# RMSNorm with SiLU on one core: framework-placed waits, a ring of 96 rows and 2 MB transfers in place of a critical section with hand-placed waits and 1 MB transfers

## The chip, the cores and the metric

The kernel runs on 1 core of one Trainium2 chip. Four of its engines appear below: ACT (ScalarE) and DVE (VectorE) do most of the arithmetic (120.5 and 112.0 us busy before), POOL (GpSimd) the reciprocal roots (32 of 1427 ns), and SP (SyncE) issues the transfers, which the core's 16 DMA engines carry out. The metric is device time in microseconds (us). An execution of the kernel before takes 166.9 us with a spread of about 0.3%. The "span" that a profile quotes is the measured stretch of one profiled execution, about 1.8 us shorter than the time of that run.

"1 MB" is 2^20 bytes throughout, "2 MB" 2^21.

## The reference, cut to what matters

```python
# x: (16, 1024, 512) float32, gamma: (512,) float32, eps: 1e-5
def reference(x, gamma, eps):
    rms = np.sqrt(np.mean(x ** 2, axis=-1, keepdims=True) + eps)
    x_norm = x / rms * gamma
    return (x_norm * (1.0 / (1.0 + np.exp(-x_norm)))).astype(np.float32)
```

There are 16384 rows of 2 KB, 32 MB in and 32 MB out. Every byte is read once and written once, whatever the kernel.

## The kernel before

Rows are handled in tiles of 128 partitions x 4 rows, which is 1 MB. There are 32 tiles and 20 buffers ("slots"). Everything sits in one critical section, a region in which the framework adds no waits between the instructions, so every wait and every semaphore (a counter that one engine raises and another waits for, as ACT and SyncE do with `s_swish` below) is written by hand.

```python
    n = 4
    n_act = 3
    lead = 8
    slots = 20
    T = R // (P * n)
    xv = xf.rearrange("(t p n) d -> t p n d", p=P, n=n)      # one partition: 4 rows = 8 KB in a row
    # ...
    def load(t):
        if t >= slots:
            nc.sync.wait_ge(st[t % slots], 16 * (t // slots))
        nc.sync.dma_start(out=X(t), in_=xv[t]).then_inc(ld[t % slots], 16)

    def store(t):
        nc.sync.wait_ge(s_swish, t + 1)
        nc.sync.dma_start(out=ov[t], in_=X(t)).then_inc(st[t % slots], 16)
    # ... ACT: 3 squares with row sums; DVE: 1 square, mean + eps, 4 x (x * rstd * gamma);
    # ... POOL: power -0.5; ACT: Silu on the whole tile
    with tc.tile_critical():
        for t in range(lead):
            load(t)
        for t in range(T):
            store(t)
            if t + lead < T:
                load(t + lead)
        # ... ACT:  sum_act(t), then swish(t - 2)
        # ... DVE:  sum_dve(t), mean_eps(t), then norm(t - 1)
        # ... POOL: root(t)
        for s in range(slots):
            nc.sync.wait_ge(st[s], 16 * ((T - 1 - s) // slots + 1))
```

SyncE (SP) issues all big transfers from one queue: 8 loads first, then store, load, store, load, each of 1 MB.

## Time and profile before

| | before |
|---|---|
| time, median of 4 runs beside the change | 166.87 us (166.76 to 167.04) |
| span of the profiled run | 165.0 us |
| busiest compute engine | ACT, 73% of the span |
| first DMA packet, last DMA packet (from the trace's DMA records) | 1.95 us, 162.14 us |

These are lines of the page of the kernel before. Each digit of the DMA row is the busy share of the 16 DMA engines in one fortieth of the span, in tenths; below it stands what they moved in that slice.

```profile
span 165.0 us, 713 instructions
...
DVE 112.0 (68%) x226; ACT 120.5 (73%) x225; POOL 46.4 (28%) x38
...
DMA  4999999999999999999999999999999999999990
GB/s 157 415 425 429 425 342 429 411 431 427 427 431 419 431 423 433 423 431 425 429 427 427 423 425 431 421 435 419 435 423 431 425 425 431 421 433 423 433 405 26
DMA packets 9229, 67.16 MB, mean 407 GB/s; under 512 B 1028, under 2 KB 1028, under 8 KB 1032
...
q1 hardware_dynamic: 9216, 67.11, 97.0%
```

The row of nines says that the DMA engines work from the first load to the last store. ACT and DVE have a quarter of their time or more to spare. The kernel is bound by DMA; the one sag, a dip of that rate (342 GB/s, the sixth slice), is where the first store reaches the engines.

The lines of the page on the chain that ended last, on the two largest groups on ACT, and on the transfers (count, KB, median us from issue to landing):

```profile
DMA xb<-in_x_dram 63%; ACT junk_a L86 12%; ACT xb L129 6%; DVE xb L121 5%; SPq L79 1%; SPq L75 0%; DVE aeps L107 0%; SPq L203 0%; SPq L131 0%
...
L86 ACT ACTIVATE junk_a<-xb 128x512 bf16<-128x512 f32 x96 | 59.2, 617 | 26.9 <-DMA xb<-in_x_dram 26.9
...
L129 ACT ACTIVATE xb<-xb 128x2048 f32<-128x2048 f32 x32 | 60.6, 1895 | 2.2 <-DVE xb L121 2.2
...
xb<-in_x_dram SPq DMA_DIRECT2D x32, 1024.0 KB, 23.2
out_dram<-xb SPq DMA_DIRECT2D x32, 1024.0 KB, 22.4
```

The chain that ended last is for 63% of the span the landing of loads. A transfer lands 22 to 23 us after its issue, although 1 MB takes about 2.45 us (2452 or 2453 ns from one transfer to the next in the DMA records). So some 9 MB are queued ahead (22.4 or 23.2 us over 2.45 us per MB, an estimate from the medians). As long as that stays so, I took it that no wait on ACT, DVE or SyncE reaches the total, only the DMA engines' own work, the start and the end.

SyncE's issues in order of time (start, length, what), first and last:

```profile
0.94 4.15 SPq L75 DMA_DIRECT2D xb<-in_x_dram  x8
15.29 0.35 SPq L79 DMA_DIRECT2D out_dram<-xb  x1
...
122.18 30.42 SPq L79 DMA_DIRECT2D out_dram<-xb  x8
```

```profile
L131 SPq EVENT_SEMAPHORE  x3: 17/17/28, 163.5 to 163.8; - x3
L131 SPq NOP  x2: 13/13/13, 0.7 to 163.8; - x2
L131 SPq COMPARE_BRANCH  x1: 33/33/33, 163.1 to 163.1; - x1
```

### The profile page before, as it was taken

The numbers are of one execution on the slowest core, as the hardware profiler recorded it, in microseconds if no ns is written. First come the engines' busy times: TensorE is split into PE (matmuls) and PEld (weight loads), VectorE is DVE, ScalarE is ACT, GpSimd is POOL, SyncE is SP. The second block draws the span as 40 slices with busy tenths as digits, with TensorE's granted clock in tenths as the row PEclk, the third lists the DMA queues.
The fourth block names the chain that finished last, engine by engine and source line by source line (L and its number), as shares of the span: only waits on it lengthen the run. The fifth ranks groups of instructions, "written<-read, shape, count | busy, mean of one in ns | idle before, by whom it ended". The sixth has DMA issues, their size and how long they took to land.

```text
span 165.0 us, 713 instructions
## 1 busy us (share of the span) xinstructions
DVE 112.0 (68%) x226; ACT 120.5 (73%) x225; POOL 46.4 (28%) x38
## 2 busy tenths in 40 slices
DVE  0269999999996666786666776666876666784000
ACT  3488999999977977777977758877778977777000
POOL 1053334443333311333321233312333311330000
DMA  4999999999999999999999999999999999999990
GB/s 157 415 425 429 425 342 429 411 431 427 427 431 419 431 423 433 423 431 425 429 427 427 423 425 431 421 435 419 435 423 431 425 425 431 421 433 423 433 405 26
DMA packets 9229, 67.16 MB, mean 407 GB/s; under 512 B 1028, under 2 KB 1028, under 8 KB 1032
## 3 DMA queue, kind: packets, MB, share of 16 engines
q1 hardware_dynamic: 9216, 67.11, 97.0%
q14 instruction: 5, 0.04, 0.1%
q10 hardware_dynamic: 8, 0.01, 0.0%
HBM read 33.56 MB, written 33.55 MB: 407 GB/s over the span
## 4 chain that ended last, share of the span: by engine, by line
DMA 63%; ACT 17%; issue 6%; DVE 5%; SPq 1%
DMA xb<-in_x_dram 63%; ACT junk_a L86 12%; ACT xb L129 6%; DVE xb L121 5%; SPq L79 1%; SPq L75 0%; DVE aeps L107 0%; SPq L203 0%; SPq L131 0%
## 5 line engine op out<-in xcount | busy, mean ns | idle before, releaser
L121 DVE SCALAR_TENSOR_TENSOR xb<-xb,rstd,gamma_sb 128x512 f32<-128x512 f32 x128 | 87.4, 745 | 0.0
L86 ACT ACTIVATE junk_a<-xb 128x512 bf16<-128x512 f32 x96 | 59.2, 617 | 26.9 <-DMA xb<-in_x_dram 26.9
L114 POOL TENSOR_TENSOR rstd<-aeps,neg_half 128x4 f32<-128x4 f32 x32 | 45.7, 1427 | 99.4 <-DVE aeps L107 99.4
L129 ACT ACTIVATE xb<-xb 128x2048 f32<-128x2048 f32 x32 | 60.6, 1895 | 2.2 <-DVE xb L121 2.2
L97 DVE CUSTOM_DVE_ANT_0 junk_v<-xb 128x512 bf16<-128x512 f32 x32 | 22.0, 689 | 8.7 <-DMA xb<-in_x_dram 6.8
L107 DVE TENSOR_SCALAR aeps<-ms 128x4 f32<-128x4 f32 x32 | 5.4, 170 | 29.6 <-ACT junk_a L86 28.9
L86 ACT ACTIVATION_READ_ACCUMULATOR junk_a<-xb 128x1 f32 x96 | 17.9, 186 | 0.0
L146 ACT ACT_TABLE_LOAD x1 | 1.3, 1283 | 2.6 <-issue 2.6
L97 DVE DVE_READ_ACCUMULATOR2_ANT ms<- 128x1 f32 x32 | 2.6, 82 | 0.0
L162 DVE STREAM_SHUFFLE gamma_sb<-gamma 128x512 f32<-128x512 f32 x1 | 0.7, 717 | 0.0
L141 POOL MEMSET gamma<- 128x512 f32 x1 | 0.5, 524 | 0.5 <-PEq L203 0.5
L189 POOL MEMSET const-float32-0.0<- 128x1 f32 x1 | 0.1, 99 | 0.2 <-issue 0.2
L189 POOL MEMSET const-uint8-127<- 128x1 uint8 x1 | 0.1, 102 | 0.0
L147 POOL MEMSET neg_half<- 128x4 f32 x1 | 0.1, 102 | 0.0
L189 POOL MEMSET const-bfloat16-1.0<- 128x1 bf16 x1 | 0.1, 101 | 0.0
L189 POOL MEMSET const-float32-1.0<- 128x1 f32 x1 | 0.1, 98 | 0.0
L162 DVE LOAD_MASK_SELECT gamma_sb<-gamma x1 | 0.0, 13 | 0.0
## 6 DMA issues: line engine op xcount, KB each, us to landing
xb<-in_x_dram SPq DMA_DIRECT2D x32, 1024.0 KB, 23.2
out_dram<-xb SPq DMA_DIRECT2D x32, 1024.0 KB, 22.4
gamma<-in_gamma_dram ACTq DMA_DIRECT2D x1, 8.0 KB
```

The source lines that it names most:

```text
L79: nc.sync.dma_start(out=ov[t], in_=X(t)).then_inc(st[t % slots], 16)
L86: ins = nc.scalar.activation(out=junk_a[:, j, :], in_=X(t)[:, j, :], func=AF.Square, accum_out=ms[:, t, j : j + 1],)
L97: ins = nc.vector.tensor_tensor_reduce(out=junk_v[:, j, :], in0=X(t)[:, j, :], in1=X(t)[:, j, :], scale=1.0, scalar=0.0, op0=ALU.mult, op1 ...
L107: nc.vector.tensor_scalar(out=aeps[:, t, :], in0=ms[:, t, :], scalar1=inv_d, scalar2=eps_f, op0=ALU.mult, op1=ALU.add,).then_inc(s_aeps, 1)
L114: nc.gpsimd.tensor_tensor(out=rstd[:, t, :], in0=aeps[:, t, :], in1=neg_half[:], op=ALU.pow).then_inc(s_rstd, 1)
L121: ins = nc.vector.scalar_tensor_tensor(out=X(t)[:, j, :], in0=X(t)[:, j, :], scalar=rstd[:, t, j : j + 1], in1=gamma_sb[:], op0=ALU.mult, ...
L129: nc.scalar.activation(out=X(t), in_=X(t), func=AF.Silu).then_inc(s_swish, 1)
L141: nc.gpsimd.memset(gamma4[:], 0.0).then_inc(s_const, 1)
L146: nc.scalar.preload_act_table_set("silu_and_others")
L147: nc.gpsimd.memset(neg_half[:], -0.5).then_inc(s_half, 1)
L162: nc.vector.stream_shuffle(gamma_sb[:], gamma4[:], [0] * 32).then_inc(s_gamma, 1)
L189: nc = _bacc.Bacc("TRN2", target_bir_lowering=False, num_devices=1)
```

## The change

Its intent: let the framework place the waits (in the order in which the program is written, with no critical section), so that the hand-made semaphores go; make transfers larger (2 MB, a partition's run of 16 KB) while compute stays in pieces of 1 MB; keep 96 rows per partition in one ring; keep all transfers on SyncE.

```diff
-    n = 4
-    n_act = 3
-    lead = 8
-    slots = 20
+    sizes = [4, 4] + [8] * 15
+    ring = 96
+    ahead = 32
+    cn = 4
+    n_act = 3
...
     def load(t):
-        if t >= slots:
-            nc.sync.wait_ge(st[t % slots], 16 * (t // slots))
-        nc.sync.dma_start(out=X(t), in_=xv[t]).then_inc(ld[t % slots], 16)
+        nc.sync.dma_start(out=buf(t), in_=dram(xf, t))
 
     def store(t):
-        nc.sync.wait_ge(s_swish, t + 1)
-        nc.sync.dma_start(out=ov[t], in_=X(t)).then_inc(st[t % slots], 16)
+        nc.sync.dma_start(out=dram(of, t), in_=buf(t))
...
-    with tc.tile_critical():
+    with tc.manual_schedule():
...
+        while rows_loaded < ahead:
+            load(loaded)
+            ...
+        for k in range(K + 2):
+            if k < K:
+                sums(k)
+                root(k)
...
+            if 1 <= k <= K:
+                norm(k - 1)
+            if k >= 2:
+                swish(k - 2)
+                while stored < len(tiles) and ends[stored] <= k - 1:
+                    store(stored)
+                    stored += 1
+                    if loaded < len(tiles):
+                        load(loaded)
+                        loaded += 1
...
-        for s in range(slots):
-            nc.sync.wait_ge(st[s], 16 * ((T - 1 - s) // slots + 1))
```

Each direction now has 2 transfers of 1 MB and 15 of 2 MB. The order of instructions on ACT, DVE and POOL is the same as before.

More of the change, by code (lines that the diff above doesn't have):

```diff
@@ L27 @@
     R, D = xf.shape
-    n = 4
+    sizes = [4, 4] + [8] * 15
+    ring = 96
+    ahead = 32
+    cn = 4
     n_act = 3
-    lead = 8
-    slots = 20
-    T = R // (P * n)
-    assert T * P * n == R, (R, n)
-    xv = xf.rearrange("(t p n) d -> t p n d", p=P, n=n)
-    ov = of.rearrange("(t p n) d -> t p n d", p=P, n=n)
+    N = sum(sizes)
+    assert N * P == R, (N, R)
+    tiles = []
+    done = 0
+    for sz in sizes:
+        assert done % ring + sz <= ring
+        tiles.append((done * P, sz, done % ring))
+        done += sz
@@ L39 @@
+    chunks = [r for _, sz, at in tiles for r in range(at, at + sz, cn)]
+    K = len(chunks)
     pool = ctx.enter_context(tc.tile_pool(name="all", bufs=1))
-    xb = pool.tile([P, slots, n, D], fp32, name="xb")
+    junk_pool = ctx.enter_context(tc.tile_pool(name="junk", bufs=1))
+    xb = pool.tile([P, ring, D], fp32, name="xb")
     gamma4 = pool.tile([P, D], fp32, name="gamma4")
     gamma_sb = pool.tile([P, D], fp32, name="gamma_sb")
-    junk_a = pool.tile([P, n, D], bf16, name="junk_a")
@@ L44 @@
-    junk_v = pool.tile([P, n, D], bf16, name="junk_v")
-    neg_half = pool.tile([P, n], fp32, name="neg_half")
-    ms = pool.tile([P, T, n], fp32, name="ms")
-    aeps = pool.tile([P, T, n], fp32, name="aeps")
-    rstd = pool.tile([P, T, n], fp32, name="rstd")
+    neg_half = pool.tile([P, cn], fp32, name="neg_half")
+    ms = pool.tile([P, K, cn], fp32, name="ms")
+    aeps = pool.tile([P, K, cn], fp32, name="aeps")
+    rstd = pool.tile([P, K, cn], fp32, name="rstd")
     inv_d = 1.0 / float(D)
@@ L51 @@
     eps_f = float(eps)
-    ld = [tc.alloc_semaphore(f"ld{s}") for s in range(slots)]
-    st = [tc.alloc_semaphore(f"st{s}") for s in range(slots)]
-    g_ld = tc.alloc_semaphore("g_ld")
-    s_const = tc.alloc_semaphore("s_const")
-    s_half = tc.alloc_semaphore("s_half")
-    s_gamma = tc.alloc_semaphore("s_gamma")
-    s_sum_a = tc.alloc_semaphore("s_sum_a")
-    s_sum_v = tc.alloc_semaphore("s_sum_v")
-    s_aeps = tc.alloc_semaphore("s_aeps")
-    s_rstd = tc.alloc_semaphore("s_rstd")
-    s_norm = tc.alloc_semaphore("s_norm")
@@ L64, with dram, buf @@
-    s_swish = tc.alloc_semaphore("s_swish")
-    def X(t):
-        return xb[:, t % slots]
-    def landed(eng, t):
-        eng.wait_ge(ld[t % slots], 16 * (t // slots + 1))
+    def dram(ap, t):
+        first, sz, _ = tiles[t]
+        return ap[first : first + P * sz].rearrange("(p n) d -> p n d", n=sz)
+    def buf(t):
+        _, sz, at = tiles[t]
+        return xb[:, at : at + sz, :]
     def load(t):
-        if t >= slots:
-            nc.sync.wait_ge(st[t % slots], 16 * (t // slots))
-        nc.sync.dma_start(out=X(t), in_=xv[t]).then_inc(ld[t % slots], 16)
+        nc.sync.dma_start(out=buf(t), in_=dram(xf, t))
@@ L77, in store @@
     def store(t):
-        nc.sync.wait_ge(s_swish, t + 1)
-        nc.sync.dma_start(out=ov[t], in_=X(t)).then_inc(st[t % slots], 16)
-    def sum_act(t):
-        landed(nc.scalar, t)
-        if t > 0:
-            nc.scalar.wait_ge(s_sum_a, t)
-        for j in range(n_act):
-            ins = nc.scalar.activation(
-                out=junk_a[:, j, :], in_=X(t)[:, j, :], func=AF.Square,
-                accum_out=ms[:, t, j : j + 1],
-            )
-        ins.then_inc(s_sum_a, 1)
-    def sum_dve(t):
-        landed(nc.vector, t)
-        if t > 0:
-            nc.vector.wait_ge(s_sum_v, t)
-        for j in range(n_act, n):
-            ins = nc.vector.tensor_tensor_reduce(
-                out=junk_v[:, j, :], in0=X(t)[:, j, :], in1=X(t)[:, j, :],
-                scale=1.0, scalar=0.0, op0=ALU.mult, op1=ALU.add,
-                accum_out=ms[:, t, j : j + 1],
-            )
-        ins.then_inc(s_sum_v, 1)
@@ L104, in mean_eps, with sums @@
-    def mean_eps(t):
-        nc.vector.wait_ge(s_sum_a, t + 1)
-        nc.vector.wait_ge(s_sum_v, t + 1)
+        nc.sync.dma_start(out=dram(of, t), in_=buf(t))
+    def sums(k):
+        for j in range(cn):
+            row = xb[:, chunks[k] + j, :]
+            if j < n_act:
+                junk = junk_pool.tile([P, D], bf16, name=f"junk_a{j}")
+                nc.scalar.activation(
+                    out=junk[:], in_=row, func=AF.Square,
+                    accum_out=ms[:, k, j : j + 1],
+                )
+            else:
+                junk = junk_pool.tile([P, D], bf16, name=f"junk_v{j}")
+                nc.vector.tensor_tensor_reduce(
+                    out=junk[:], in0=row, in1=row,
+                    scale=1.0, scalar=0.0, op0=ALU.mult, op1=ALU.add,
+                    accum_out=ms[:, k, j : j + 1],
+                )
@@ L107, in mean_eps, with root @@
+    def root(k):
         nc.vector.tensor_scalar(
-            out=aeps[:, t, :], in0=ms[:, t, :], scalar1=inv_d, scalar2=eps_f,
+            out=aeps[:, k, :], in0=ms[:, k, :], scalar1=inv_d, scalar2=eps_f,
             op0=ALU.mult, op1=ALU.add,
-        ).then_inc(s_aeps, 1)
-    def root(t):
-        nc.gpsimd.wait_ge(s_aeps, t + 1)
+        )
         nc.gpsimd.tensor_tensor(
-            out=rstd[:, t, :], in0=aeps[:, t, :], in1=neg_half[:], op=ALU.pow
-        ).then_inc(s_rstd, 1)
-    def norm(t):
-        nc.vector.wait_ge(s_rstd, t + 1)
-        for j in range(n):
-            ins = nc.vector.scalar_tensor_tensor(
-                out=X(t)[:, j, :], in0=X(t)[:, j, :], scalar=rstd[:, t, j : j + 1],
+            out=rstd[:, k, :], in0=aeps[:, k, :], in1=neg_half[:], op=ALU.pow
+        )
@@ L123, in norm @@
+    def norm(k):
+        for j in range(cn):
+            row = xb[:, chunks[k] + j, :]
+            nc.vector.scalar_tensor_tensor(
+                out=row, in0=row, scalar=rstd[:, k, j : j + 1],
                 in1=gamma_sb[:], op0=ALU.mult, op1=ALU.mult,
             )
-        ins.then_inc(s_norm, 1)
-    def swish(t):
-        nc.scalar.wait_ge(s_norm, t + 1)
-        nc.scalar.activation(out=X(t), in_=X(t), func=AF.Silu).then_inc(s_swish, 1)
-    with tc.tile_critical():
-        for t in range(lead):
-            load(t)
-        for t in range(T):
-            store(t)
-            if t + lead < T:
-                load(t + lead)
-        nc.gpsimd.memset(gamma4[:], 0.0).then_inc(s_const, 1)
-        nc.scalar.wait_ge(s_const, 1)
-        nc.scalar.dma_start(
-            out=gamma4[0:P:32, :], in_=gamma.partition_broadcast(4)
-        ).then_inc(g_ld, 16)
-        nc.scalar.preload_act_table_set("silu_and_others")
-        nc.gpsimd.memset(neg_half[:], -0.5).then_inc(s_half, 1)
-        nc.gpsimd.wait_ge(s_half, 1)
-        for t in range(T + 2):
-            if t < T:
-                sum_act(t)
-            if t >= 2:
-                swish(t - 2)
-        for t in range(T + 1):
-            if t < T:
-                sum_dve(t)
-                mean_eps(t)
-            if t == 0:
-                nc.vector.wait_ge(g_ld, 16)
-                nc.vector.stream_shuffle(gamma_sb[:], gamma4[:], [0] * 32).then_inc(s_gamma, 1)
-            if t == 1:
-                nc.vector.wait_ge(s_gamma, 1)
-            if t >= 1:
-                norm(t - 1)
-        for t in range(T):
-            root(t)
-        for s in range(slots):
-            nc.sync.wait_ge(st[s], 16 * ((T - 1 - s) // slots + 1))
@@ new lines, in swish @@
+    def swish(k):
+        rows = xb[:, chunks[k] : chunks[k] + cn, :]
+        nc.scalar.activation(out=rows, in_=rows, func=AF.Silu)
+    with tc.manual_schedule():
+        nc.gpsimd.memset(gamma4[:], 0.0)
+        nc.gpsimd.memset(neg_half[:], -0.5)
+        nc.scalar.dma_start(out=gamma4[0:P:32, :], in_=gamma.partition_broadcast(4))
+        nc.scalar.preload_act_table_set("silu_and_others")
+        loaded = 0
+        rows_loaded = 0
+        while rows_loaded < ahead:
+            load(loaded)
+            rows_loaded += tiles[loaded][1]
+            loaded += 1
+        ends = []
+        e = 0
+        for _, sz, _ in tiles:
+            e += sz // cn
+            ends.append(e)
+        stored = 0
+        for k in range(K + 2):
+            if k < K:
+                sums(k)
+                root(k)
+            if k == 0:
+                nc.vector.stream_shuffle(gamma_sb[:], gamma4[:], [0] * 32)
+            if 1 <= k <= K:
[7 more added lines that the diff above has]
+                        load(loaded)
+                        loaded += 1
```

## The prediction

> **What bounds the kernel now.** The DMA engines, from end to end. The page's slice rows show DMA at 9 tenths or more in all slices but the first and last, at 405 to 435 GB/s, with one dip (342) near 21 to 24 us, where the first store reaches the engines. ACT is busy 73%, DVE 68%, POOL 28%. In the DMA records of the trace the first packet starts at 1.95 us, the last ends at 162.1, and the packets of one engine (a 16th) add up to 160.3 us: no holes. The rest is 1.9 us before and 2.8 us after. SP's own waits (113.5 us for Silu) are harmless: a store takes 22 us from issue to landing, so some 9 MB are queued ahead.
>
> So the time can change only by cost per packet, by a queue that runs dry, or at head and tail.
>
> **What a packet costs.** 8192 packets of 8192 bytes take 309 ns (median), the four of 2048 bytes (gamma) 84 ns, a 4-byte semaphore packet 9 ns. A line through these is about 9 ns plus bytes at 27.3 GB/s per engine (437 GB/s on 16)[...]. Estimate for 16384 bytes: 609 ns instead of 2 x 309.
>
> **What the change does.**
> - 64 transfers of 1 MB become 4 of 1 MB and 30 of 2 MB, whose contiguous run per partition is 16 KB. If that is one packet, each engine handles 272 large packets instead of 512: 240 x 9 ns = 2.2 us saved. 30 fewer semaphore packets: 0.27 us. Both lie wholly on the critical path.
> - No critical section: a no-op and a branch before the first load (issued at 0.94 us) go: 0.1 us.
> - The framework recycles 8 DMA semaphores, so each DMA waits for the one 8 before it: up to 16 MB in flight. Squares also wait for the earlier writer of their scratch tile, on the same engine. The order on ACT, DVE and POOL is unchanged.
> - Store t now needs the sums of both chunks of load t+1: about 7.7 us of ACT (2 x 1.93 + 2 x 1.9) after it lands, against 9.8 us of DMA per pair of 2 MB.
>
> **Does the queue run dry?** The initial 8 MB last until 21 us. Load 2 lands at about 13.4; store 0 issues at 17.4, store 1 at 21, store 2 at 28.7 (work queued until 36), store 3 at 36.4 (queued until 46); then the backlog grows to about 9 MB. At the end, load 16 lands with three stores ahead of store 15; the last Silu ends 13.4 us later, against about 17.6 us of stores. I expect no holes.
>
> **Prediction:** 166.9 - 2.2 - 0.3 - 0.1, about 164.2 us; 163.3 to 166.5. Chances: faster by over 2% 0.13, same 0.82, slower 0.05.
>
> **What would show it.** About 4350 large data packets, most of 16384 bytes at 609 to 611 ns, 544 semaphore packets; DMA at 9 tenths throughout, near 430 GB/s; first load issued near 0.85 us; the dip at the first store still there; compute durations unchanged; ACT idle waiting for loads.
>
> **What would make it wrong.** Runs cut into 8 KB packets: only 0.4 us gained (166.5). The 8-semaphore rotation or the later store 0 drains the queue around 21 to 30 us: 1 to 3 us lost, slices under 400 GB/s. Self-waits on ACT use up its 2 us of slack per pair. A longer closing drain.

## More of the kernel before

The end of the kernel, from the listings by source line: the waits of the last loop (line 172), the exit of the critical section (line 131) and the first of the framework's own closing instructions (line 203). Columns: count, duration in ns (least, median, most), first and last start in us.

```profile
L172 SPq EVENT_SEMAPHORE  x10: 17/28/28, 160.1 to 163.0; - x10
```

```profile
L203 SPq DRAIN  x3: 7/7/7, 163.9 to 164.2; - x3
...
L203 POOLq EVENT_SEMAPHORE_RANGE_CLEAR  x1: 333/333/333, 164.3 to 164.3; - x1
```

The last packet is through at 162.14 us. The waits after that run one by one to 163.0, the branch out of the critical section follows at 163.1, its own round of waits takes until 163.8, and only then, at 163.9, does the framework's drain begin. The span ends at 165.0, 2.83 us after the last packet.

## The result, and the profile after

| | before | after |
|---|---|---|
| time, median (range), 4 runs each | 166.87 us (166.76 to 167.04) | 165.69 us (165.19 to 165.83) |
| ratio, 95% interval | | 0.9923 (0.9901 to 0.9946) |

A ratio here is the mean time of one kernel's fast runs over that of the other's fast runs of the same rounds, so it is not quite the ratio of the medians beside it. The kernel is about 0.8% faster; 1.6% was predicted, with a range of 163.3 to 166.5 us that does hold the time. Of the 2.7 us forecast 1.2 came, so more than half of the gain is missing, and what was gained did not come from where the prediction had it, as follows.

The same lines of the page after:

```profile
span 163.9 us, 638 instructions
...
DVE 111.1 (68%) x226; ACT 119.3 (73%) x225; POOL 46.4 (28%) x38
...
DMA  5999999999999999999999999999999999999991
GB/s 174 448 408 444 440 308 428 428 410 438 416 436 424 432 428 432 420 432 428 428 428 440 428 428 432 432 418 434 432 436 424 428 420 428 432 436 432 424 412 48
DMA packets 4908, 67.15 MB, mean 410 GB/s; under 512 B 548, under 2 KB 548, under 8 KB 552
...
q1 hardware_dynamic: 4896, 67.11, 97.1%
```

The transfers did become half as many packets (4908 in all instead of 9229), and the DMA row is full again, so the queue did not run dry. The sag at the first store is deeper (308 instead of 342 GB/s). In the last slice the engines are busy one tenth and move 48 GB/s: a few DMA engines are still at work when the others have nothing left.

```profile
DMA xb<-in_x_dram 60%; ACT junk_a L80 14%; ACT xb L111 13%; DVE xb L104 3%; SPq L73 1%; SPq L70 0%; DVEq L178 0%; DVE aeps L93 0%; ACTq L80 0%
...
L80 ACT ACTIVATE junk_a<-xb 128x512 bf16<-128x512 f32 x96 | 59.0, 615 | 28.2 <-DMA xb<-in_x_dram 28.2
...
L111 ACT ACTIVATE xb<-xb 128x2048 f32<-128x2048 f32 x32 | 60.6, 1894 | 1.8 <-DVE xb L104 1.8
...
xb<-in_x_dram SPq DMA_DIRECT2D x15, 2048.0 KB, 25.5
out_dram<-xb SPq DMA_DIRECT2D x15, 2048.0 KB, 25.6
```

Compute is unchanged (squares 615 ns against 617, Silu 1894 against 1895), and a transfer of 2 MB still lands 25 us after its issue.

```profile
0.74 2.56 SPq L70 DMA_DIRECT2D xb<-in_x_dram  x5
16.96 0.35 SPq L73 DMA_DIRECT2D out_dram<-xb  x1
...
116.27 35.82 SPq L73 DMA_DIRECT2D out_dram<-xb  x5
```

The first load is issued at 0.74 us instead of 0.94, and the first stores come at 16.96 and the following ones close to the times that the prediction worked out (17.4, 21, 28.7, 36.4; the trace has 16.96, 20.60, 27.87, 35.15).

```profile
L178 SPq EVENT_SEMAPHORE  x7: 17/28/10762, 152.1 to 163.9; - x7
...
L178 SPq DRAIN  x3: 7/7/7, 163.2 to 163.5; - x3
...
L178 POOLq EVENT_SEMAPHORE_RANGE_CLEAR  x1: 95/95/95, 163.5 to 163.5; - x1
```

The end: the last packet is through at 162.60 us, the framework's waits of SyncE follow one another only three more times, and its drain begins at 163.2. The span ends at 163.9, 1.33 us after the last packet instead of 2.83.

### Where the time went: the trace's DMA records

The trace has a record of each DMA packet (start, duration, size, queue). They can be summed by a few lines of code, and they answer what the page can't. The records don't name the DMA engine. But every transfer leaves 128 data packets (256 when a partition's run is cut in two, as in frame_2mb_8k) and 16 semaphore packets of 4 bytes (8192 and 1024 for the 64 transfers before, 4352 and 544 for the 34 after), and from transfer to transfer most of these 16 move on by the same step (2452 or 2453 ns in 85% of the cases before). So I take them as one per engine, after 8 (or 16) data packets each, and their times as showing how far the engines are apart. The table has these numbers:

```
                          first    last transfer, semaphore packets    span end minus
                          packet   fastest   median   slowest engine   last packet
before                     1.95    160.29    161.01    162.13          2.83
after                      1.75    159.40    159.96    162.60          1.33
after minus before        -0.20     -0.89              +0.47          -1.50

distance of slowest from fastest:  before 1.84    after 3.20
one engine's time per 2 MB where nothing disturbs it:  before 4906 ns (two transfers)    after 4862 ns
```

On 16 engines together 2 MB in 4906 ns are 427 GB/s, and 2 MB in 4862 ns are 431.

The span changed by -1.03 us: -0.20 at the head, -0.69 in the work of the fastest engine, +1.36 because the slowest engine lags further behind it, -1.50 at the end. The prediction had -0.1, about -2.45 for both engine terms together, and 0 at the end.

In neither trace does an engine that is held up catch up: put in order of time, no semaphore packet of these two traces follows its counterpart of the transfer before by less than 2452 ns for 1 MB or 4862 ns for 2 MB. So the slowest engine, at 162.13 and 162.60 us, decides. What holds them up are single packets that take far longer than their like: 611 ns is the median of a 16 KB packet after, but 122 packets of the run took over 20 ns more than their kind, up to 1.1 us more. This excess I call stall time, divided by 16 so that it is us per engine. Before, the stalls sit at the start, at the first store, and (0.14 of the 0.16 us after 26 us) within 0.7 us of an instruction fetch packet. After, there are stalls every 10 us or so until the last load: 0.93 us per engine after 26 us, and 0.91 of that lies in the last 2.6 us of a load that a store follows (such a load takes 4.9 us, so this is also the time from some 2 us after it began; the quads below tell the two apart).

Stall times come from durations of records, which the end of this document shows to be a poor measure of a packet's cost. The semaphore packets check them: the mean of the last 16 is at 161.04 us before and at 160.36 after. A start 0.20 us earlier and packets cheaper by 1.3 us (worked out below) would have brought it to 159.5, so 0.8 us per engine was lost; the stall times of the whole runs differ by about 1.1.

### The profile page after: what moved, and what is told of

Its sections match the earlier page's. It is cut to its first block, busy times and chain, and to the rows that moved or that the text cites. A ratio compares the mean times of both kernels' runs of the same rounds, so it can differ in the third digit from the quotient of the medians.

```text
span 163.9 us, 638 instructions
## 1 busy us (share of the span) xinstructions
DVE 111.1 (68%) x226; ACT 119.3 (73%) x225; POOL 46.4 (28%) x38
## 2 busy tenths in 40 slices
DMA packets 4908, 67.15 MB, mean 410 GB/s; under 512 B 548, under 2 KB 548, under 8 KB 552
## 4 chain that ended last, share of the span: by engine, by line
DMA 60%; ACT 27%; DVE 3%; SPq 1%; issue 0%; DVEq 0%; ACTq 0%
DMA xb<-in_x_dram 60%; ACT junk_a L80 14%; ACT xb L111 13%; DVE xb L104 3%; SPq L73 1%; SPq L70 0%; DVEq L178 0%; DVE aeps L93 0%; ACTq L80 0%
## 5 line engine op out<-in xcount | busy, mean ns | idle before, releaser
L111 ACT ACTIVATE xb<-xb 128x2048 f32<-128x2048 f32 x32 | 60.6, 1894 | 1.8 <-DVE xb L104 1.8
## 6 DMA issues: line engine op xcount, KB each, us to landing
xb<-in_x_dram SPq DMA_DIRECT2D x15, 2048.0 KB, 25.5
```

The source lines that it names most:

```text
L111: nc.scalar.activation(out=rows, in_=rows, func=AF.Silu)
```

## The experiments

Theory A: the gains at head and end belong to the framework, the lag of single engines to the 2 MB transfers. Rival B: the lag comes with the framework's waits and order. A second question was which property of a 2 MB transfer it is: the 16 KB packet, or that the engines move 2 MB in one direction before they turn round. A row of transfers in one direction is called a stretch below, the change of direction a turn.

The table gives, for each kernel, the time (median and range), the ratio to the kernel before, and from the profiled run's DMA records the distance of the slowest from the fastest engine at the last transfer ("lag"; the last 16 semaphore packets where there are two queues), the time from the last packet to the end of the span ("end"), and the stall time per engine from 15 to 36 us (the first turn from loads to stores) and after 36 us. The table counts every data packet that took at least 6 ns more than the median of its size, not 20 as above. The expectations below count "later stalls" from 26 us on. Each row's last four columns are from one trace; the profiled runs of frame_1mb_pairs (165.47 us) and frame_2mb_8k (165.84) were 0.4 and 0.5 us faster than their medians, so what they show of lag and stalls may be less than is usual.

```
kernel              us (range)                ratio   lag   end   stalls 15-36  after 36 us
before              166.87 (166.76 to 167.04)  1      1.84  2.83      0.69         0.08
after               165.69 (165.19 to 165.83) 0.9923  3.20  1.33      1.31         0.62
after_again         165.86 (165.85 to 166.26) 0.9933  3.35  1.35      1.32         0.72
frame_1mb           164.96 (164.78 to 165.11) 0.9884  1.86  1.34      1.02         0.13
crit_2mb            166.34 (165.92 to 166.85) 0.9966  2.87  1.94      1.41         0.64
frame_2mb_8k        166.30 (165.38 to 166.94) 0.9965  1.92  1.32      0.88         0.76
frame_1mb_pairs     165.86 (165.42 to 166.27) 0.9937  2.20  1.20      0.90         0.54
frame_1mb_quads     166.11 (165.89 to 166.46) 0.9950  2.92  1.22      0.62         0.98
frame_1mb_48        164.90 (164.70 to 165.87) 0.9887  1.82  1.20      0.52         0.13
split_2mb           164.76 (164.60 to 164.88) 0.9868  0.16  1.35      0.79         0.39
split_1mb           180.42 (180.21 to 180.97) 1.0818
pool_stores_2mb     164.04 (163.99 to 164.28) 0.9821  1.42  1.88      0.69         0.11
act_loads_2mb       163.51 (163.49 to 163.65) 0.9788  1.59  1.34      0.55         0.28
act_loads_2mb_8k    164.61 (164.45 to 164.66) 0.9854  1.41  1.34      0.51         0.06
```

All of them computed the right result. The twelve experiments follow in the order in which they ran; edits are against the changed kernel unless said otherwise.

### frame_1mb: the framework, with 1 MB transfers

```diff
-    sizes = [4, 4] + [8] * 15
+    sizes = [4] * 32
```

> The changed kernel with 32 transfers of 1 MB each way (8 KB packets), everything else of the framework version kept. Theory A: the framework's version gains 1.75 us at head and close (0.2 + 1.55), and the lost gain comes from the 2 MB transfers, whose packets stall single engines so that the slowest engine ends 3.2 us after the fastest instead of 1.8. Then here: 165.1 us, engines 2.45 us per MB, slowest engine about 1.8 us or less behind the fastest. Rival B: the stalls come with the framework's waits and order: slowest engine about 3 us behind, 166.3 us or more.

Measured: 164.96 us, ratio 0.9884 (0.9871 to 0.9897), lag 1.86 us, end 1.34 us, 4906 ns per 2 MB. Theory A holds, to 0.15 us. Undoing the 2 MB transfers makes the changed kernel faster. The profiled spans differ by 1.7 us (165.0 to 163.3), and 0.22 us at the head and 1.49 at the end make it up; the body takes as long as before.

### crit_2mb: the critical section, with 2 MB transfers

Edit of the kernel before (cut): loads and stores by `sizes`, one semaphore per transfer, ring of 96 rows.

```diff
-    lead = 8
-    slots = 20
+    sizes = [4, 4] + [8] * 15
+    ring = 96
+    lead = 5
...
-        nc.sync.dma_start(out=X(t), in_=xv[t]).then_inc(ld[t % slots], 16)
+        nc.sync.dma_start(out=buf(i), in_=dram(xf, i)).then_inc(ld[i], 16)
...
-        nc.sync.wait_ge(s_swish, t + 1)
-        nc.sync.dma_start(out=ov[t], in_=X(t)).then_inc(st[t % slots], 16)
+        nc.sync.wait_ge(s_swish, ends[i])
+        nc.sync.dma_start(out=dram(of, i), in_=buf(i)).then_inc(st[i], 16)
...
-        for s in range(slots):
-            nc.sync.wait_ge(st[s], 16 * ((T - 1 - s) // slots + 1))
+        for s in range(M):
+            nc.sync.wait_ge(st[s], 16)
```

> The kernel before (critical section, own semaphores) with the changed kernel's transfers: 2 of 1 MB and 15 of 2 MB each way, ring of 96 rows, 8 MB ahead. Theory A (stalls come with 2 MB transfers, head and close with the critical section): engines 2.43 us per MB, slowest engine about 3 us behind the fastest, close about 2.3 to 2.8 us, 166.7 to 167.2 us. Rival B (stalls come with the framework): slowest engine 1.8 us behind, 165.5 us.

Measured: 166.34 us, lag 2.87 us, stalls after 36 us 0.64, 4862 ns per 2 MB. The lag comes without the framework, so rival B falls. The time is 0.4 us under the range that A gave, because the end is shorter than I allowed for: 1.94 us against 2.83. Here the last store's semaphore is waited for last; before, eight more waits followed it, from 162.49 to 163.03 us (0.55 us in the trace). Most of the other 0.34 us is the gap after the branch out of the critical section (0.15 us against 0.43), which I have no reason for. The framework's own end is shorter by another 0.61 us (1.33), with no exit from a critical section at all.

The time fell by 0.56 us (166.90 to 166.34) although the end alone gives 0.89, so here the 2 MB transfers lost some 0.3 us (0.1 to 0.6 with the interval of the ratio, 0.9950 to 0.9982). In the framework they lose 0.73 to 0.90 us (164.96 to 165.69 and 165.86, from different sessions; by the ratios 0.65 to 0.82).

### frame_2mb_8k: 2 MB transfers in 8 KB packets

```diff
-        return ap[first : first + P * sz].rearrange("(p n) d -> p n d", n=sz)
+        rows = ap[first : first + P * sz]
+        return rows.rearrange("(h p n) d -> p h (n d)", p=P, n=4)
...
-        return xb[:, at : at + sz, :]
+        return xb[:, at : at + sz, :].rearrange("p (h n) d -> p h (n d)", n=4)
```

> The changed kernel with the same 2 MB transfers whose rows are laid out so that each contiguous run is 8 KB (two runs per partition). If the stalls come with the 16 KB packet: slowest engine 1.8 us behind or less, 4.89 us per 2 MB (only the semaphore packet saved), 164.8 to 165.3 us. If they come with the length of a stretch of loads or stores (2 MB in one direction): slowest engine 3 us behind, about 166.5 us.

```profile
DMA packets 8748, 67.15 MB, mean 409 GB/s; under 512 B 548, under 2 KB 548, under 8 KB 552
```

8748 packets: the transfers are those of the changed kernel, the packets those before. Measured: 166.30 us, stalls after 36 us 0.76. The stalls stay, so they don't belong to the 16 KB packet. The lag was not 3 us but 1.92: here the stalls were spread over more engines, and the fastest was itself at 160.81 us. The undisturbed time per 2 MB is 4900 ns, against 4906 with two semaphore packets: one of those costs 6 ns.

### frame_1mb_pairs: 1 MB transfers, two stores and then two loads

```diff
-    sizes = [4, 4] + [8] * 15
+    sizes = [4] * 32
...
-                while stored < len(tiles) and ends[stored] <= k - 1:
-                    store(stored)
-                    stored += 1
-                    if loaded < len(tiles):
-                        load(loaded)
-                        loaded += 1
+                if (k - 1) % 2 == 0:
+                    for _ in range(2):
+                        store(stored)
+                        stored += 1
+                    for _ in range(2):
+                        if loaded < len(tiles):
+                            load(loaded)
+                            loaded += 1
```

> frame_1mb with two stores issued after each other, then two loads: 1 MB transfers, 8 KB packets, but stretches of 2 MB in one direction. If the stalls come with the length of a stretch in one direction: slowest engine about 3 us behind, 166.3 us. If with the packet or the transfer: as frame_1mb, 165.1 us.

Measured: 165.86 us, 0.90 us slower than frame_1mb; stalls after 36 us 0.54 against 0.13. Packets, transfers, semaphores and framework are those of frame_1mb, only the order differs. So the stalls come with stretches of 2 MB in one direction. Lag and time stayed below what I expected (2.20 us and 165.86 instead of about 3 and 166.3).

### split_2mb: stores from ACT's queue

```diff
     def store(t):
-        nc.sync.dma_start(out=dram(of, t), in_=buf(t))
+        nc.scalar.dma_start(out=dram(of, t), in_=buf(t))
```

> The changed kernel with its stores issued from ACT's queue instead of SyncE's, so that loads and stores sit in two queues[...]. If the stalls come from long stretches of loads between stores (frame_1mb_pairs: 0.90 us of later stalls per engine against 0.22 in frame_1mb), they go: slowest engine under 2 us behind the fastest, 16 KB packets keep their 4.86 us per 2 MB, 164.2 us or a little less. If the stalls belong to any turn between loads and stores, there are more of them: 166 us or more.

Measured: 164.76 us, 0.9 us faster than the changed kernel, though not the 164.2 expected. The page shows why not; its slices end in 310, 450, 322 and 257 GB/s:

```profile
GB/s 175 434 434 442 402 362 446 410 428 416 434 418 438 442 414 430 446 422 422 446 426 426 434 438 422 426 442 430 418 434 438 418 430 446 418 426 310 450 322 257
...
q1 hardware_dynamic: 2448, 33.56, 49.0%
q10 hardware_dynamic: 2456, 33.56, 48.3%
```

Loads now run ahead by themselves (a load of 2 MB lands 42.4 us after its issue, against 25.5), and near the end the stores come at the pace of ACT (from 111 to 150 us it issues one every 7.8 us, and 2 MB take 4.86 us), with gaps between them: about 2.4 us per engine without a packet before the fastest engine ended, against 0.5 in the changed kernel.

### split_1mb: the same with 1 MB transfers

The edits of frame_1mb and split_2mb together.

> frame_1mb with stores from ACT's queue. If long stretches cause the stalls, little is left to gain at 1 MB: 164.6 to 165.0 us against 164.96. If every turn costs, it is slower than frame_1mb.

```profile
DMA  5999999999999999999999999999995555556696
GB/s 195 431 419 402 367 428 428 426 424 430 426 430 428 426 426 428 428 426 428 424 431 426 428 426 428 426 430 426 424 397 240 235 235 235 235 246 255 264 380 264
```

Measured: 180.42 us, 8% slower. Both expectations are wrong, for a reason that neither was about: from the 31st slice on the engines move some 240 GB/s. In the trace of the changed kernel the transfers signal 8 semaphores in rotation, and an issue waits for the transfer 8 before it in the program; I take it that the framework does the same here. With 1 MB transfers in two queues that would couple loads, stores and compute: the trace's waits show SyncE 70.4 us waiting for earlier loads and 15.5 us for stores to land, and ACT idle 39.7 us for loads, so that the last stores come one by one behind ACT's compute. That the semaphores are the cause is argued from these waits, not tested. The run says nothing on turns.

### frame_1mb_quads and frame_1mb_48: stretches of 4 MB, and their control

frame_1mb_quads is frame_1mb_pairs with 4 in place of 2 and `ahead = 48` (12 MB loaded first); frame_1mb_48 is frame_1mb with `ahead = 48` alone.

> frame_1mb with four stores, then four loads (stretches of 4 MB in one direction, 8 KB packets), 12 MB loaded ahead so that the queue can't run dry. If the stall is a thing of stretch length: at least the 0.90 us of later stalls per engine of frame_1mb_pairs though the turns are half as many, 166 us or more. If it is a cost per turn at a given length over 1 MB: about half of pairs, 165.4 us.

> Control for the quads: frame_1mb with 12 MB loaded ahead instead of 8. Loads and stores alternate by 1 MB as before. Expected 165.0 us as frame_1mb; if the stall before the first store belongs to the end of the stretch of loads, it moves from 20 to 23 us to about 30 to 33 us; if it belongs to that time, it stays.

Measured: 166.11 us and 164.90 us. After 36 us the quads stall for 0.98 us per engine, in five stretches of loads (0.03 to 0.36 in each); the pairs had 0.54 in about 11, the control and frame_1mb 0.13 in about 21 (and instruction fetches are in all of these). So a stretch of loads between stores costs on average roughly 0.2, 0.05 and at most 0.01 us per engine at 4, 2 and 1 MB: more than in proportion.

The quads also show where in a stretch the stalls sit. Their loads last about 10 us: 0.70 of the 0.98 us lies 1.4 to 3 us after the loads began, 7 us or so before the stores, and only 0.16 in the last 2.6 us. So these later stalls are not tied to the turn from loads to stores, as the traces with stretches of 2 MB alone would suggest.

The first sag moves with the length of the first stretch. These are windows of 3 us (start and end, DVE, ACT and POOL busy with instruction counts, a clock of no use here, DMA share, GB/s), first of the kernel before, then of frame_1mb_48:

```profile
20.00:23.00 3.00, 2.89 (x7) 3.00 (x7) 1.44 (x1) 1.00 0.95 328
...
30.00:33.00 3.00, 2.88 (x7) 3.00 (x7) 1.06 (x1) 1.00 1.01 410
```
```profile
20.00:23.00 3.00, 2.89 (x7) 3.00 (x6) 1.44 (x1) 1.00 1.00 418
...
30.00:33.00 3.00, 2.88 (x7) 3.00 (x7) 1.44 (x1) 1.00 0.93 341
```

With 8 MB loaded ahead the sag (328 GB/s) lies at 20 to 23 us, with 12 MB it lies at 30 to 33 us (341), and at 20 to 23 there is none. This sag belongs to the end of the first stretch of loads, not to that time. It isn't deeper for 12 MB than for 8 (stalls from 15 to 36 us are 0.52 against 1.02), so the first sag doesn't grow with the length of the stretch as the later stalls do.

### act_loads_2mb: loads after the first five from ACT's queue

```diff
     def load(t):
-        nc.sync.dma_start(out=buf(t), in_=dram(xf, t))
+        (nc.sync if t < 5 else nc.scalar).dma_start(out=buf(t), in_=dram(xf, t))
```

> The changed kernel with all loads after the first five issued from ACT's queue, stores still from SyncE. Loads are issued right after the Silu of tile t, so they are paced as in the changed kernel (split_2mb let them run ahead, and its last four slices sagged to 310, 450, 322, 257 GB/s when the stores waited for ACT). If that sag was the loss of split_2mb: no sag, later stalls about 0.4 us per engine as in split_2mb, slowest engine 2.4 us behind or less, 163.0 to 164.0 us. If two queues bring nothing but the mixing already seen: 164.8 us as split_2mb.

```profile
span 161.9 us, 637 instructions
...
DMA  5999999999999999999999999999999999999993
GB/s 170 443 425 445 421 429 387 411 441 411 419 441 417 437 441 417 437 437 413 445 437 409 449 427 417 443 429 421 445 421 429 441 425 429 441 417 433 445 413 130
...
q1 hardware_dynamic: 3168, 41.94, 61.1%
q10 hardware_dynamic: 1736, 25.17, 36.7%
```

Measured: 163.51 us, ratio 0.9788 (0.9775 to 0.9801) to the kernel before, as expected: no sag at the end, and none of 300 GB/s at the first store. From 60 to 119 us every interval of 1 us has packets of both queues, so loads and stores come finely mixed. That this is why the stalls are fewer (0.28 us after 36 us against 0.72 in after_again, of the same session) is argued from this and from the next experiment, not isolated. The fastest engine ends at 158.95 us and the slowest at 160.53, against 159.39 and 162.74 in after_again. This version beats both the kernel before and the changed one.

### pool_stores_2mb: stores from POOL's queue

```diff
-        nc.sync.dma_start(out=dram(of, t), in_=buf(t))
+        nc.gpsimd.dma_start(out=dram(of, t), in_=buf(t))
```

> The changed kernel with its stores issued from the Pool engine[...]. Loads are not paced by stores, only by the ring and the recycled semaphores. If a second queue of any kind removes the stalls: later stalls of 0.4 us per engine or less, 164 to 165 us.[...]

```profile
q0 software_dynamic: 2448, 33.56, 48.4%
```

Measured: 164.04 us, within the 164 to 165 us expected; stalls after 36 us 0.11. The page counts 4909 packets against the changed kernel's 4908, the 17 issues keep POOL busy for 593 ns each, and a reciprocal root takes 1435 ns against 1427. A second queue of another kind brings much the same, though here the stores do not pace the loads (one of 2 MB lands 61.1 us after its issue), with an end that is 0.5 us longer (1.88 us).

### after_again: the changed kernel, unedited

> The changed kernel once more, unedited, for the spread of its stalls: 165.2 to 165.9 us, slowest engine 2 to 3.5 us behind the fastest, later stalls near 1 us per engine, close 1.3 us, 4.86 us per 2 MB.

Measured: 165.86 us (165.85 to 166.26), lag 3.35 us, stalls 1.32 and 0.72, end 1.35, 4862 ns per 2 MB. The readings of the first profile repeat.

### act_loads_2mb_8k: the price of a packet where stalls are few

The edits of act_loads_2mb and frame_2mb_8k together.

> act_loads_2mb with contiguous runs of 8 KB instead of 16 KB: the same transfers, queues and semaphores, 240 more data packets per engine. Measures what a packet costs where stalls are few. The records of undisturbed stretches give 4900 ns per 2 MB with 8 KB runs (frame_2mb_8k) and 4862 ns with 16 KB runs (changed kernel), 4.75 ns per packet saved: then 163.5 + 240 x 4.75 ns = 164.6 us. The prediction's 9 ns per packet (from the packets' recorded durations) would give 165.7 us.

Measured: 164.61 us, 1.10 us over act_loads_2mb (163.51, timed in an earlier session; the ratios to the kernel before are 0.9854 and 0.9788, whose difference of 0.66% is 1.1 us). A packet saved was worth about 4.6 ns here (1.10 us / 240), not 9: 240 x 9 ns would be 1.3%, and the intervals of the ratios (0.9837 to 0.9870, 0.9775 to 0.9801) lie at most 0.95% apart.

## Why the prediction was wrong

**What held.** The bound (DMA, with no holes), the 16 KB packets (3840 of them at a median of 611 ns, as 609 to 611 was predicted), 544 semaphore packets, unchanged compute, the times of the first stores, and the sag at the first store. The 8 recycled semaphores (in the trace each serves 4 or 5 of the 34 transfers) and the extra waits on ACT (93 of the 96 squares wait for ACT's own semaphore) cost nothing that shows: the DMA row stays full.

**First wrong step: "240 x 9 ns = 2.2 us saved" and "30 fewer semaphore packets: 0.27 us".** The mechanism is right and the term is mis-sized by two. I read the cost of a packet from the durations of the records. But records of neighbouring packets on an engine overlap: sixteen of 309 ns and one of 9 ns make 4953 ns, and the engine is through after 4900 (frame_2mb_8k). The step from one transfer's end to the next is the honest measure: 38 ns less for 8 packets fewer, 4.75 ns each, and 6 ns for a semaphore packet. That gives 240 x 4.75 + 30 x 6 ns = 1.3 us instead of 2.45. act_loads_2mb_8k against act_loads_2mb confirms it with whole times.

**Second wrong step: the sum leaves out the engines' stalls.** The prediction added up the average engine and treated the sag at the first store as a constant. With 2 MB stretches single engines are held up in most stretches of loads, the slowest ends 3.20 instead of 1.84 us after the fastest, and the fastest too loses part of its gain (0.69 us left of 1.3). This took back 2.0 us (1.36 and 0.6), more than the packets had brought. The pairs show that the order alone brings such stalls, frame_2mb_8k that the large packet isn't needed for it, crit_2mb that the framework isn't.

**Third wrong step: no gain at the end.** The only thing that I said of the end was that "a longer closing drain" might come. The trace of before had the answer in its last 3 us: nine waits that end one by one after the last store has landed, a branch, and the round of waits that leaves the critical section. The change removes 1.50 us: 0.42 of the waits, 0.82 of the branch and the exit, and 0.30 of the framework's own closing instructions (among them POOL's clearing of semaphores, 95 ns against 333), less 0.04 us by which the first wait ends later. That is more than the net gain of the whole change (1.18 us); frame_1mb, the framework alone, gained 1.94. The head was 0.20 instead of 0.1.

So the change is faster for a reason that I had not counted, and its declared improvement, the larger transfer, is by itself a loss in this order of issue.

**What stays open.** Why single engines are held up in a stretch of loads, and why longer stretches make it worse, is not shown. The first sag lies at the end of the loads, the later stalls of the quads mostly about 2 us after the loads began, so it is open which turn matters, and whether both have one cause. The records don't tell the reading of a packet from its writing. Nor do they tell why frame_1mb stalls more at the first turn than the kernel before (1.02 against 0.69 us) with the same sequence of transfers, or which engines are hit.

## What to carry to other kernels

In a kernel bound by DMA, count the head and the end in the trace as carefully as the body: here 2.83 us followed the last packet before and 1.33 after, and the 1.50 us between them were more than the 1.3 us that the cheaper packets were worth. Take the cost of a packet from the step between completions, not from the durations of records (4.75 ns against 9 here), and look at the slowest DMA engine, not the average (here it ended 3.20 us after the fastest). When loads and stores share one queue, a larger transfer also means a longer stretch in one direction, and here that cost more than the larger packet brought (165.69 and 165.86 us against 164.96 with 1 MB transfers). With loads and stores on two queues the larger packet did pay here (163.51 us against 164.61 with packets of 8 KB). But look at what the waits become: the same step with 1 MB transfers took 180.42 us.
